# Up projections of one SwiGLU layer by Strassen's seven products instead of eight

## The chip, the cores and the metric

The kernel runs on one core of a Trainium2 chip. The metric is the device time of one execution in microseconds (us); smaller is better. Five engines work side by side, each through its own list of instructions in order, and meet at semaphores: PE (TensorE, matrix products, with its weight loads shown as PEld), DVE (VectorE), ACT (ScalarE), POOL (GpSimd) and SP (SyncE, which here only issues DMAs).

## The reference

Two trunk layers work on 256 context tokens and 512 latent tokens of 1024 channels. Each layer is a half-step SwiGLU, a mixer (attention beside a convolution in the first layer, a two-way RWKV-7 scan in the second) and another half-step SwiGLU. The change concerns the first SwiGLU of the second layer, for all 768 tokens:

```python
def half_ffn(x, shift, scale, gate, w1, w3, w2):
    h = modulate(x, shift, scale)
    return x + 0.5 * gate * ((jax.nn.silu(h @ w1) * (h @ w3)) @ w2)
```

`w1` and `w3` are 1024 x 2816, `w2` is 2816 x 1024.

## The kernel before

All activations lie with channels on the 128 lanes and tokens along the row, so 1024 channels are 8 tiles (k) and the 2816 inner channels 22 blocks of 128 (f). The tokens form two groups, CTX (columns 0 to 255) and LAT (256 to 767).

Products are made in three parts. Every operand is split into a high part, rounded by a copy to a shorter float type, and a low part, the rest; `mmk` (L435) issues high x high, high x low and low x high into the same PSUM bank. For a weight tile (128 x 1024) the split is a copy on ACT (`whi`, L202) and a subtraction on DVE (`wlo`, L209). The pool of weights holds four raw tiles and four split pairs (`W_RAW`, `W_SP`). PSUM has eight banks, four called `psa` and four called `psb`.

In `ffn` (L469), `f1` makes one block f: 48 products with a `w1` tile (8 k x 3 parts x 2 groups), SiLU on ACT (L476), 48 products with the `w3` tile, and for each group the gate: a product on DVE (`fs`, L484), a rounded copy on ACT (`ghi`, L485) and the rest on DVE (`glo`, L486). `f2` brings a chunk of blocks down: for each of eight output tiles m and each group `down` (L503) multiplies the chunk's gated blocks with `w2` and adds the result to the residual on DVE (L511). Chunks are 4, 4, 4, 4, 2 and 4 blocks; a chunk's `f2` runs after the first block of the next chunk. The very first two blocks of the layer run k by k while the normalisation still delivers (`first_block`).

The order of everything is written out by hand: each engine executes its instructions in the order in which the Python emits them. `w_next` (L211) emits the split of later weight tiles ahead of the block that now starts. `ticks` (L181) emits one piece of background work at a time; in this layer there is none before the change.

Of the kernel before, what the change touches and what calls it, by code (L numbers as in the profile page):

```python
# [7 lines left out]
F32 = mybir.dt.float32  # L8
F32R = mybir.dt.float32r
# [12 lines left out]
CHUNKS = (4, 4, 4, 4, 2, 4)  # L22
CTX = (0, NCTX, 1)
# [6 lines left out]
class Cols:  # L30
    def __init__(self):
        self.at = {}
        self.n = 0
# [56 lines left out]
def layout(inp):  # L90
# [10 lines left out]
    parts, f0 = [], 0  # L101
    for cf in CHUNKS:
        t = w2[:, :, f0:f0 + cf].reshape(2, 2, cf, 128, cf, 8 // cf, 128)
        parts.append(t.transpose(0, 1, 4, 3, 5, 2, 6).reshape(2, 2, -1))
        f0 += cf
    a["w2"] = np.ascontiguousarray(np.concatenate(parts, 2))
# [33 lines left out]

class K:
# [10 lines left out]
    # ---------- pools  # L152
# [33 lines left out]
    # ---------- weights  # L186
# [24 lines left out]
    def w_next(self, key, live=0):  # L211
        i = self.w_i
        assert self.w_items[i][0] == key, (self.w_items[i][0], key)
        last = min(i + self.W_SP - 1 - live - 1, len(self.w_items) - 1)
        while self.w_s <= max(last, i):
            while self.w_d <= min(self.w_s + self.W_RAW - 1, len(self.w_items) - 1):
# [4 lines left out]
        while self.w_d <= min(self.w_s + self.W_RAW - 1, len(self.w_items) - 1):  # L221
            self.w_dma(self.w_d)
            self.w_d += 1
# [30 lines left out]
    # ---------- adaLN  # L254
# [17 lines left out]
    def ada_first(self):  # L272
        """shift and scale of the first FFN, half of the channels at a time: every product on the tensor engine, four column groups at once"""
# [53 lines left out]
    # ---------- norm + modulation: h = x * rsqrt(mean(x^2) + eps) * scale + shift  # L327
# [89 lines left out]
    # ---------- SwiGLU  # L417
    def ffn_items(self, l, i):
        A = self.A
        it = []  # L420
        off = f = 0
# [47 lines left out]
    def ffn(self, l, i, groups, h, post=None, first=None):  # L469
        nc = self.nc  # L470
        gd = 2 if i == 0 else 8
        gs = {}

# [14 lines left out]
        def f1(f, nt):  # L488
# [6 lines left out]
            w = self.w_next(("w3", l, i, f))  # L495
            pss = [self.psa() for g in groups]
# [27 lines left out]
        for c, cf in enumerate(CHUNKS):  # L524
            q = 0
            if c == 0 and first is not None:
# [54 lines left out]
                q = 2  # L581
            while q < cf:
# [10 lines left out]
        c, f0, cf = pend  # L593
        if post is None:
            f2(c, f0, cf)
            return None
# [29 lines left out]
    # ---------- MLA || conv mixer  # L626
# [18 lines left out]
    def conv_tap(self, t, k, split=False):  # L645
        """one tap of the depthwise convolution; zeros part the two streams in cin"""
# [20 lines left out]
    def mla(self, h, norm_lat):  # L667
# [54 lines left out]
        # the first two blocks of the convolution's input run while the latent tokens are normalised  # L722
# [34 lines left out]
        # latent projections: kv, q, rope key  # L757
# [58 lines left out]
        # token-major q, k, v  # L816
# [11 lines left out]
        def rot(dst, src, w, t, n, eng):  # L828
            """gain and rotation of n tables' tokens; src and dst [128, n, 32], t the first table, or None where nothing turns"""
# [27 lines left out]
        def prep(p):  # L857
            """closures: transposes, split and row maxima of one pair of heads"""
# [129 lines left out]
        self.plan(self.wout_items() + self.ffn_items(0, 1) + self.ffn_items(1, 0) + self.rwkv_items())  # L988
# [72 lines left out]
        def fin(p):  # L1061
            """closures: one over the sums, and the outputs split"""
# [181 lines left out]
        # output projection  # L1244
# [16 lines left out]
        # the attention's half of the rows first; the first NH blocks of the latent tokens go with the context's  # L1261
# [45 lines left out]
    # ---------- RWKV-7 mixer (second layer)  # L1307
# [22 lines left out]
    def rw_sum(self, kt, g):  # L1330
        """the sum of a token's neighbours"""
# [10 lines left out]
    def rw_diff(self, kt, g):  # L1342
        """half the sum, less the token"""
# [1394 lines left out]
```

## Time and profile before

| quantity | value |
|---|---|
| median of 3 timed runs | 3436.01 us (3432.27 to 3439.86) |
| span of the profiled execution | 3438.3 us, within the timed runs |
| matrix products on PE | 21064 |
| mean granted PE clock | 0.947 |

The profile covers one execution from the first to the last instruction; its span is the time that the sums below refer to, 2.3 us above the median. A line of a group names the source line, the engine, the operation, the output and input tiles by the program's names, the shape, how often it ran and its mean duration. In a line of the timeline the first number is the start in us from the span's start, the second the duration.

### The profile page before, as it was taken

The page shows a single profiled execution, that of the slowest core. Times are in us where ns is not written, and L with a number is a line of the kernel's source. Part 1 is how long each engine was busy: PE and PEld are TensorE (multiplying, and loading weights), DVE is VectorE, ACT ScalarE, POOL GpSimd, SP SyncE. Part 2 cuts the span into 40 slices and gives each one's busy share as a digit, 9 for nine tenths or more (in the row PEclk, how much of TensorE's full clock was granted, in tenths as well). Part 3 has the DMA queues.
Part 4 walks back from the last instruction along what each step waited for, and adds up shares of the span by engine and source line. Part 5 has one row for each costly group of instructions (what it writes and reads, how often), then busy time and mean ns, then how long its engine had stood idle before and what let it go on. Part 6 is the DMA issues. An engine that isn't in the chain of part 4 may idle for free. (4 is left out here: it accounts for less than half of the span.)

```text
span 3438.3 us, 51746 instructions
## 1 busy us (share of the span) xinstructions
PE 3168.0 (92%) x21064; PEld 2636.7 (77%) x21064; DVE 2069.5 (60%) x3246; ACT 1141.4 (33%) x2060; POOL 663.6 (19%) x464
## 2 busy tenths in 40 slices
PE   7999999988989999999999999998786477789999
PEld 6888888874578888888888888776554367678887
DVE  5877734798667776555333343637899775663443
ACT  4122213455543211124122113335564245532222
POOL 1000001356320000002000001215787142230000
PEclk9999999999999999999999999999777689989999
DMA  6444311200133444431111111322587788733222
GB/s 242 146 150 147 132 68 62 78 25 1 47 108 129 141 140 150 146 111 56 68 62 62 62 68 62 109 89 95 149 213 201 186 186 184 165 127 103 98 98 80
DMA packets 251374, 390.59 MB, mean 114 GB/s; under 512 B 67328, under 2 KB 136576, under 8 KB 251136
## 3 DMA queue, kind: packets, MB, share of 16 engines
q1 hardware_dynamic: 251136, 387.28, 36.7%
q8 instruction: 166, 2.72, 0.3%
q14 instruction: 72, 0.59, 0.1%
HBM read 323.24 MB, written 63.96 MB: 113 GB/s over the span
## 5 line engine op out<-in xcount | busy, mean ns | idle before, releaser
L233 PE MATMUL psa<-hhi,whi 128*128 128x512 f32 (+1 forms) x2584 | 893.5, 346 | 6.0 <-ACT whi L202 3.9
L233 PE MATMUL psa<-hlo,whi 128*128 128x512 f32 (+1 forms) x2584 | 894.8, 346 | 2.5 <-POOL hlo L385 2.2
L233 PE MATMUL psa<-hhi,wlo 128*128 128x512 f32 (+1 forms) x2584 | 892.1, 345 | 0.0
L209 DVE TENSOR_TENSOR wlo<-wraw,whi 128x1024 fp32r<-128x1024 f32 (+3 forms) x300 | 366.9, 1225 | 450.5 <-ACT whi L202 450.5
L233 PEld LDWEIGHTS psa<-hhi,whi 128*128 128x128 f32 x2584 | 490.0, 190 | 69.7 <-ACT whi L202 3.9
L233 PEld LDWEIGHTS psa<-hlo,whi 128*128 128x128 f32 x2584 | 489.2, 189 | 67.1 <-POOL hlo L385 4.1
L233 PEld LDWEIGHTS psa<-hhi,wlo 128*128 128x128 f32 x2584 | 489.6, 189 | 61.3
L202 ACT CAST whi<-wraw 128x1024 fp32r<-128x1024 f32 (+2 forms) x345 | 344.6, 1009 | 337.1 <-PE psb L233 198.2
L233 PE MATMUL psb<-ghi,whi 128*128 128x512 f32 (+1 forms) x1232 | 425.6, 345 | 1.4 <-DVE xb L511 0.9
L233 PE MATMUL psb<-glo,whi 128*128 128x512 f32 (+1 forms) x1232 | 424.8, 345 | 0.0
L233 PE MATMUL psb<-ghi,wlo 128*128 128x512 f32 (+1 forms) x1232 | 424.5, 345 | 0.0
L342 POOL TENSOR_TENSOR nacc<-nacc,nsq 128x512 f32<-128x512 f32 (+1 forms) x50 | 56.2, 1125 | 1579.0 <-ACT nsq L338 1574.0
L476 ACT ACTIVATE fs<-psa 128x512 f32<-128x512 f32 (+1 forms) x152 | 77.3, 509 | 576.3 <-PE psa L233 576.2
L485 ACT CAST ghi<-fs 128x512 fp32r<-128x512 f32 (+1 forms) x154 | 81.7, 530 | 552.7 <-DVE fs L484 552.7
L233 PEld LDWEIGHTS psb<-ghi,whi 128*128 128x128 f32 x1232 | 231.9, 188 | 32.8 <-issue 2.2
L233 PEld LDWEIGHTS psb<-ghi,wlo 128*128 128x128 f32 x1232 | 232.0, 188 | 30.0
L233 PEld LDWEIGHTS psb<-glo,whi 128*128 128x128 f32 x1232 | 231.8, 188 | 30.0 <-DVE glo L486 0.3
L484 DVE TENSOR_TENSOR fs<-fs,psa 128x512 f32<-128x512 f32 (+1 forms) x149 | 85.1, 571 | 200.5 <-PE psa L233 197.5
L511 DVE SCALAR_TENSOR_TENSOR xb<-psb,mod,xb 128x256 f32<-128x256 f32 (+1 forms) x192 | 115.7, 614 | 124.5 <-PE psb L233 124.4
L268 DVE CUSTOM_DVE_ANT_0 adaj<-adat,sc,vec 128x512 bf16<-128x512 f32 x224 | 167.9, 750 | 14.7 <-DMA adat<-ada 9.1
L268 DVE CUSTOM_DVE_ANT_0 adaj<-adat,sc,mod 128x512 bf16<-128x512 f32 x224 | 167.9, 750 | 5.9 <-DMA adat<-ada 0.3
L233 PE MATMUL psb<-rhs,lhs 96*32 96x64 f32 (+1 forms) x2560 | 81.1, 241 | 70.4 <-DVE prod L2104 21.4
(398 smaller groups left out, 4907.7 us busy)
## 6 DMA issues: line engine op xcount, KB each, us to landing
wraw<-w SPq DMA_DIRECT2D x264, 512.0 KB
adat<-ada SPq DMA_DIRECT2D x256, 256.0 KB
la_d<-AR SPq DMA_DIRECT2D x32, 384.0 KB
kb_d<-KT SPq DMA_DIRECT2D x16, 768.0 KB
lg_d<-G SPq DMA_DIRECT2D x32, 384.0 KB
lhs<-la_d SPq DMA_DIRECT2D x48, 256.0 KB
lhs<-lg_d SPq DMA_DIRECT2D x48, 256.0 KB
kb<-kb_d SPq DMA_DIRECT2D x48, 256.0 KB
```

The costliest lines, as they stand in the source:

```text
L202: nc.scalar.copy(hi, raw)
L209: nc.vector.tensor_tensor(lo, raw, hi, ALU.subtract)
L233: self.last = self.nc.tensor.matmul(ps, lhsT=lhsT, rhs=rhs, start=start, stop=stop)
L268: nc.vector.tensor_tensor_reduce(out=junk, in0=t, in1=self.sc[cd][hf], scale=1.0, scalar=o if hf else self.col("ada_b", l * 72 + j), op0=A ...
L342: (eng or nc.gpsimd).tensor_tensor(st["acc"], st["acc"], sq, ALU.add)
L476: nc.scalar.activation(s, ps[:, 0:grp[1]], AF.Silu)
L484: nc.vector.tensor_tensor(s, s, ps[:, 0:n], ALU.mult)
L485: nc.scalar.copy(ghi[:, t0:t0 + n], s)
L511: nc.vector.scalar_tensor_tensor(xs, ps[:, 0:n], self.modc(l, gd, m, cd), xs, ALU.mult, ALU.add)
```

## The change

The 18 blocks from f = 4 on are taken in nine pairs. For a pair and one of `w1`, `w3` the product has two halves of inner channels (the two blocks), two halves of input channels (k 0 to 3 and 4 to 7) and two halves of tokens (columns 0 to 383 and 384 to 767, slices tA and tB). The class `Strassen` forms it from seven products of half size in place of eight. Each of the seven is 12 matrix products (4 k x 3 parts) of 384 columns into one `psa` bank, and is named in `ORDER` after its token operand.

- Token operands: `sums` adds and subtracts the four quarters of the activations once and splits the results; S2, S3 and A22 go to new tiles `ht2`, `ht3`, `ht4` as background work during blocks 2 and 3, S1 overwrites part of the activations during the first products (`one`).
- Weight operands: per pair and matrix, four subtractions or additions of 128 x 512 on DVE (L226 to L229) change the raw tiles, and the splits (L234, L237) make three and a half 1024-wide units instead of two. `ahead` emits one unit ahead of each product when fewer than four are held.
- Results: `pair` combines the seven products on DVE (seven additions of 384 columns, `add`, L358) and by one copy on ACT (L369); `out` applies SiLU and the gate to each of four quarters of the pair (L345, L353 to L355).
- Down projection: chunks are now pairs of blocks (`PAIRS`), and the eight steps m of the previous pair's down projection stand among the 14 products of a pair, behind the products listed in `STEPS`. The same `w2` bytes are packed two blocks to a tile (array `w2p`); two `w2` units are split per pair.

The rows below are instructions as they stand in the two programs, with the semaphores on which each waits in brackets. Before, on DVE, this is a block's `w3` half and the first three steps of the down projection behind it (`xb`: the residual tiles, two rows a step, CTX and LAT):

```order
L209 TENSOR_TENSOR wlo<-wraw,whi 128x1024 [waits DMAHW1_49,Activation_49]
L484 TENSOR_TENSOR fs<-fs,psa 128x256 [waits PE_49]
L486 TENSOR_TENSOR glo<-fs,ghi 128x256 [waits Activation_49]
L484 TENSOR_TENSOR fs<-fs,psa 128x512 [waits PE_49]
L486 TENSOR_TENSOR glo<-fs,ghi 128x512 [waits Activation_49]
L209 TENSOR_TENSOR wlo<-wraw,whi 128x1024 [waits DMAHW2_49,Activation_49]
L511 SCALAR_TENSOR_TENSOR xb_7779<-psb,mod_83,xb_7779 128x256 [waits PE_49]
L511 SCALAR_TENSOR_TENSOR xb_7779<-psb,mod_83,xb_7779 128x512 [waits PE_49]
L511 SCALAR_TENSOR_TENSOR xb_7781<-psb,mod_83,xb_7781 128x256 [waits PE_49]
L511 SCALAR_TENSOR_TENSOR xb_7781<-psb,mod_83,xb_7781 128x512 [waits PE_49]
L209 TENSOR_TENSOR wlo<-wraw,whi 128x1024 [waits DMAHW3_49,Activation_49]
L511 SCALAR_TENSOR_TENSOR xb_7783<-psb,mod_83,xb_7783 128x256 [waits PE_49]
```

After, on DVE, the `w3` half of a pair in the run of pairs. The first row adds product S2; `wlo` is a `w2` unit of the next pair; then come the addition for S3, the evictions of a step, two additions for S1 with gate product and rest (`glo`), and the next step's evictions:

```order
L358 TENSOR_TENSOR e<-psa,e 128x384 [waits PE_49]
L237 TENSOR_TENSOR wlo<-wraw,whi 128x1024 [waits DMAHW6_49,PE_49,Activation_49]
L358 TENSOR_TENSOR e<-psa,e 128x384 [waits DVE_49]
L792 SCALAR_TENSOR_TENSOR xb_7789<-psb,mod_83,xb_7789 128x256
L792 SCALAR_TENSOR_TENSOR xb_7789<-psb,mod_83,xb_7789 128x512
L358 TENSOR_TENSOR e<-psa,e 128x384 [waits DVE_49]
L358 TENSOR_TENSOR e<-psa,e 128x384
L353 TENSOR_TENSOR e<-e 128x384 [waits DVE_49]
L355 TENSOR_TENSOR glo<-e,ghi 128x384 [waits Activation_49]
L792 SCALAR_TENSOR_TENSOR xb_7791<-psb,mod_83,xb_7791 128x256
L792 SCALAR_TENSOR_TENSOR xb_7791<-psb,mod_83,xb_7791 128x512
```

The rest of the same half: the four sums of the next weights, the addition for A22 with its gate, a `wlo`, and the addition for S4 with its gate:

```order
L226 TENSOR_TENSOR ws_15418<-wraw 128x512 [waits DMAHW5_49]
L227 TENSOR_TENSOR wraw<-wraw 128x512 [waits DVE_49]
L228 TENSOR_TENSOR wraw<-ws_15418,wraw 128x512 [waits DVE_49]
L229 TENSOR_TENSOR wraw<-wraw 128x512 [waits DVE_49]
L358 TENSOR_TENSOR e<-psa,e 128x384
L353 TENSOR_TENSOR e<-e 128x384 [waits DVE_49]
L355 TENSOR_TENSOR glo<-e,ghi 128x384 [waits Activation_49]
L237 TENSOR_TENSOR wlo<-wraw,whi 128x1024 [waits PE_49]
L358 TENSOR_TENSOR e<-psa,e 128x384
L353 TENSOR_TENSOR e<-e 128x384 [waits DVE_49]
L355 TENSOR_TENSOR glo<-e,ghi 128x384 [waits Activation_49]
```

Against before, the additions and the gates have come between the splits, and each group of rows stands behind a `wlo` row that waits for PE.

Before, on PE, the end of a block's LAT products and the start of the down projection:

```order
L233 MATMUL psa<-hlo_13643,whi 128x512
L233 MATMUL psa<-hhi_13635,wlo 128x512
L233 MATMUL psb<-ghi,whi 128x256 [waits Activation_49]
L233 MATMUL psb<-glo,whi 128x256
L233 MATMUL psb<-ghi,wlo 128x256 [waits DVE_49]
L233 MATMUL psb<-ghi,whi 128x256
```

After, on PE, the end of product A12 of a pair (`hhi`, 384 columns) and the first step of the previous pair's down projection; the two `psb` groups are CTX and LAT, and within a group the two blocks of the pair:

```order
L506 MATMUL psa<-hhi_13635,wlo 128x384
L506 MATMUL psb<-ghi,whi 128x256 [waits DVE_49,Activation_49]
L506 MATMUL psb<-glo,whi 128x256
L506 MATMUL psb<-ghi,wlo 128x256
L506 MATMUL psb<-ghi,whi 128x256 [waits Activation_49]
L506 MATMUL psb<-glo,whi 128x256 [waits DVE_49]
L506 MATMUL psb<-ghi,wlo 128x256
L506 MATMUL psb<-ghi,whi 128x512 [waits Activation_49]
L506 MATMUL psb<-glo,whi 128x512 [waits DVE_49]
```

Before, the gate for which the first step waits belongs to a block with another whole block of products between; now the last one belongs to S4 of the pair just finished, with one step, A11 and A12 between on PE.

The diff, cut to its core (removed comments, the packing of `w2p`, the lists of items and of loads, and a smaller scratch area for DMA descriptors, which makes room in SBUF, are left out):

```diff
 CHUNKS = (4, 4, 4, 4, 2, 4)
+PAIRS = (2, 2, 2, 2, 2, 2, 2, 2, 2, 4)
...
+class Strassen:
+    PLACE = {"A11": (0, 0), "A12": (0, 1), "S2": (1, 0), "S4": (1, 1), "S3": (2, 0), "A22": (2, 1), "S1": (3, 0)}
+    ORDER = "A11", "A12", "S2", "S3", "S1", "A22", "S4"
+    STEPS = 1, 3, 4, 6, 8, 10, 11, 13
+    def __init__(self, k, l, i, groups, h, gs):
+        self.k, self.nc, self.h, self.gs = k, k.nc, h, gs
+        A = k.A
+        c0 = groups[0][0]
+        n = self.n = sum(g[1] for g in groups) // 2
+        self.tt = [slice(c0, c0 + n), slice(c0 + n, c0 + 2 * n)]
+        self.fp, self.close = k.open("fx", 1, side="right")
+        self.T = {}
+        self.mats = [(m, f) for f in range(4, NF, 2) for m in ("w1", "w3")]
...
+        self.units, self.loads = [], []
+        for j, (m, f) in enumerate(self.mats):
+            self.units += [(j, 0), (j, 1), (j, 2), (j, 3)]
+            self.loads += [((j, q), A[m][l, i, f + q].rearrange("p k m -> p (k m)")) for q in range(2)]
+            c = f // 2 - 1
+            if c < len(PAIRS) - 1:
+                key = ("w2", c, j % 2)
+                self.units.insert(len(self.units) - 3, key)
+                self.loads.append((key, w2[key[1:]]))
...
+    def split(self):
+        nc, k = self.nc, self.k
+        u = self.units[self.u]
+        self.u += 1
+        TT = nc.vector.tensor_tensor
+        if u[0] != "w2" and u[1] == 3:
+            hi = self.fp.tile([128, 512], F32R, tag="hi", bufs=1, name="shi")
+            lo = self.fp.tile([128, 512], F32R, tag="lo", bufs=1, name="slo")
+        else:
+            hi = k.wp.tile([128, 1024], F32R, tag="hi", bufs=k.W_SP, name="whi")
+            lo = k.wp.tile([128, 1024], F32R, tag="lo", bufs=k.W_SP, name="wlo")
+        self.sp[u] = hi, lo
+        drop = []
+        if u[0] == "w2":
+            x = self.raw[u]
+            drop = [u]
+        else:
+            j, q = u
+            if q == 1:
+                R0, R1 = self.raw[j, 0], self.raw[j, 1]
+                s1 = self.tmp[j] = k.tp.tile([128, 512], F32, tag="t", name="ws1")
+                TT(s1, R1[:, 0:512], R1[:, 512:1024], ALU.add)
+                TT(R1[:, 0:512], R0[:, 0:512], R1[:, 0:512], ALU.subtract)
+                TT(R0[:, 0:512], s1, R0[:, 0:512], ALU.subtract)
+                TT(R0[:, 512:1024], R0[:, 512:1024], R0[:, 0:512], ALU.subtract)
+            x = {0: self.raw.get((j, 0)), 1: self.raw.get((j, 0)), 2: self.raw.get((j, 1)), 3: self.tmp.get(j)}[q]
+            drop = {0: [], 1: [(j, 0)], 2: [(j, 1)], 3: []}[q]
+            if q == 3:
+                del self.tmp[j]
+        nc.scalar.copy(hi, x)
+        def f():
+            TT(lo, x, hi, ALU.subtract)
+            for r in drop:
+                del self.raw[r]
+        return f
+    def ahead(self):
+        self.flush()
+        self.load()
+        if self.u < len(self.units):
+            u = self.units[self.u]
+            small = [v for v in self.sp if v[1] == 3 and v[0] != "w2"]
+            if (not small) if (u[0] != "w2" and u[1] == 3) else len(self.sp) - len(small) < self.k.W_SP:
+                self.late = [self.split()]
...
+    def unit(self, u, last):
+        while self.u <= self.at[u]:
+            self.flush()
+            self.load()
+            self.late = [self.split()]
+        if self.at[u] == self.u - 1:
+            self.flush()
+        return self.sp.pop(u) if last else self.sp[u]
+    def sums(self):
...
+        def plain(kt, c):
+            t = et()
+            TT(t, hhi[kt][:, c], hlo[kt][:, c], ALU.add)
+            return t
+        def split(x, hi, lo):
+            nc.scalar.copy(hi, x)
+            TT(lo, x, hi, ALU.subtract)
+        def s1(kt):
+            tiles[kt] = [plain(kt, tA), plain(kt, tB), plain(kt + 4, tA), plain(kt + 4, tB)]
+        def s2(kt):
+            r11, r12, r21, r22 = tiles[kt]
+            TT(r11, r12, r11, ALU.subtract)
+            TT(r12, r22, r12, ALU.subtract)
+            TT(r22, r22, r11, ALU.subtract)
+            TT(r21, r21, r22, ALU.subtract)
+        def s3(kt):
+            r11, r12, r21, r22 = tiles.pop(kt)
+            for o, x in ((2, r22), (3, r12), (4, r21)):
+                t = k.slab([128, NT], F32R, f"ht{o}")
+                self.T[o, kt] = t[:, 0:n], t[:, n:2 * n]
+                split(x, *self.T[o, kt])
+        k.bg += [lambda f=f, kt=kt: f(kt) for kt in range(4) for f in (s1, s2, s3)]
+        def one(kt):
+            a, b = plain(kt, tA), plain(kt, tB)
+            TT(b, b, a, ALU.subtract)
+            split(b, hhi[kt][:, tB], hlo[kt][:, tB])
+        self.one = [lambda kt=kt: one(kt) for kt in range(4)]
...
+    def product(self, j, o):
+        k = self.k
+        u, q = self.PLACE[o]
+        hi, lo = self.unit((j, u), o in ("A12", "S1", "A22", "S4"))
+        c = slice(512 * q, 512 * q + 512)
+        w = hi[:, c], lo[:, c]
+        hi = lo = None
+        self.ahead()
+        ps = k.psa()
+        for kt in range(4):
+            k.mmk(ps[:, 0:self.n], w, kt, self.rhs(o, kt), kt == 0, kt == 3)
+        return ps
...
+    def out(self, j, blk, x):
+        nc, k = self.nc, self.k
+        m, f = self.mats[j]
+        if m == "w1":
+            nc.scalar.activation(x, x, AF.Silu)
+            self.s[blk] = x
+            return
+        s = self.s.pop(blk)
+        f += blk[0]
+        if f not in self.gs:
+            self.gs[f] = (k.slab([128, NT], F32R, "ghi"), k.slab([128, NT], F32R, "glo"))
+        hi, lo = (t[:, self.tt[blk[1]]] for t in self.gs[f])
+        nc.vector.tensor_tensor(s, s, x, ALU.mult)
+        nc.scalar.copy(hi, s)
+        nc.vector.tensor_tensor(lo, s, hi, ALU.subtract)
...
+    def pair(self, f, step):
+        at = 0
+        for m in ("w1", "w3"):
+            j = self.mats.index((m, f))
+            for o in self.ORDER:
+                ps = self.product(j, o)
+                if o == "A11":
+                    u2 = self.e()
+                    self.nc.scalar.copy(u2, ps[:, 0:self.n])
+                elif o == "A12":
+                    c11 = self.e()
+                    self.add(c11, ps, u2)
+                    self.out(j, (0, 0), c11)
+                    c11 = None
+                elif o == "S2":
+                    self.add(u2, ps, u2)
+                elif o == "S3":
+                    u3 = self.e()
+                    self.add(u3, ps, u2)
+                elif o == "S1":
+                    c22 = self.e()
+                    self.add(c22, ps, u3)
+                    self.add(u2, ps, u2)
+                    self.out(j, (1, 1), c22)
+                    c22 = None
+                elif o == "A22":
+                    self.add(u3, ps, u3)
+                    self.out(j, (1, 0), u3)
+                    u3 = None
+                else:
+                    self.add(u2, ps, u2)
+                    self.out(j, (0, 1), u2)
+                    u2 = None
+                ps = None
+                if self.one:
+                    self.one.pop(0)()
+                if step and at in self.STEPS:
+                    step(self.STEPS.index(at))
+                at += 1
+    def end(self):
+        self.flush()
+        self.T.clear()
+        self.load()
+        self.k.w_pre()()
+        self.k.w_pre()()
+        self.close()
...
             w = self.w_next(("w3", l, i, f))
+            if fast and f == 3:
+                fx.begin()
...
-        for c, cf in enumerate(CHUNKS):
+        chunks = PAIRS if fast else CHUNKS
+        w2w = []
+        def step(c, f0, m):
+            if m % 4 == 0:
+                w2w.clear()
+                w2w.append(fx.unit(("w2", c, m // 4), True))
+            for g in groups:
+                down(f0, 2, m, w2w[0], g)
+            if m == 7:
+                w2w.clear()
+                for f in range(f0, f0 + 2):
+                    del gs[f]
+        for c, cf in enumerate(chunks):
+            if fast and c > 1:
+                for f in range(f0, f0 + cf, 2):
+                    if pend:
+                        fx.pair(f, lambda m, c=pend[0], q=pend[1]: step(c, q, m))
+                    else:
+                        fx.pair(f, None)
+                    pend = None
+                pend = (c, f0, cf)
+                f0 += cf
+                continue
...
                 q = 2
+                if fast:
+                    fx.sums()
...
         c, f0, cf = pend
+        if fast:
+            fx.end()
         if post is None:
...
-        self.plan(self.wout_items() + self.ffn_items(0, 1) + self.ffn_items(1, 0) + self.rwkv_items())
+        self.plan(self.wout_items() + self.ffn_items(0, 1))
+        it, tail = self.ffn_items(1, 0, True)
+        self.plan(it)
+        self.w_stops.append(len(self.w_items))
+        self.plan(tail + self.rwkv_items())
...
-        st = self.ffn(1, 0, [CTX, LAT], h, post=self.rw_begin, first=self.hook(st0, 1, 0, h))
+        st = self.ffn(1, 0, [CTX, LAT], h, post=self.rw_begin, first=self.hook(st0, 1, 0, h), fast=True)
...
```

More of the change, by code (lines that the diff above doesn't have):

```diff
@@ L138, in layout, with load, flush, begin @@
     return a
+class Strassen:
[11 more added lines that the diff above has]
+        self.mats = [(m, f) for f in range(4, NF, 2) for m in ("w1", "w3")]
+        w2, off = {}, 0
+        for c, cf in enumerate(PAIRS):
+            for b in range(cf):
+                w2[c, b] = A["w2p"][off:off + 131072].rearrange("(p n) -> p n", p=128)
+                off += 131072
+        self.units, self.loads = [], []
[7 more added lines that the diff above has]
+                self.loads.append((key, w2[key[1:]]))
+        self.at = {u: n for n, u in enumerate(self.units)}
+        self.u = 0
+        self.raw, self.tmp, self.sp = {}, {}, {}
+        self.late = []
+        self.s = {}
+    def load(self):
+        k = self.k
+        while self.loads and len(self.raw) < k.W_RAW:
+            key, ap = self.loads.pop(0)
+            t = self.raw[key] = k.wp.tile([128, 1024], F32, tag="raw", bufs=k.W_RAW, name="wraw")
+            self.nc.sync.dma_start(out=t, in_=ap)
+        if not self.loads:
+            while k.w_d < len(k.w_items) and k.w_d - k.w_s + len(self.raw) < k.W_RAW:
+                k.w_dma(k.w_d)
+                k.w_d += 1
+    def split(self):
[33 more added lines that the diff above has]
+        return f
+    def flush(self):
+        while self.late:
+            self.late.pop(0)()
+    def ahead(self):
[6 more added lines that the diff above has]
+                self.late = [self.split()]
+    def begin(self):
+        for _ in range(2):
+            self.ahead()
[8 more added lines that the diff above has]
+    def sums(self):
+        k, nc = self.k, self.nc
+        hhi, hlo = self.h
+        n = self.n
+        tA, tB = self.tt
+        TT = nc.vector.tensor_tensor
+        tiles = {}
+        def et():
+            return self.fp.tile([128, n], F32, tag="e", bufs=7, name="e")
+        def plain(kt, c):
[25 more added lines that the diff above has]
+        self.one = [lambda kt=kt: one(kt) for kt in range(4)]
+    def rhs(self, o, kt):
+        hhi, hlo = self.h
+        tA, tB = self.tt
+        k, c = {"A11": (kt, tA), "A12": (kt + 4, tA), "S4": (kt + 4, tB), "S1": (kt, tB), "S2": (2, None), "S3": (3, None), "A22": (4, None)}[o]
+        if c is None:
+            return self.T[k, kt]
+        return hhi[k][:, c], hlo[k][:, c]
+    def product(self, j, o):
+        k = self.k
+        u, q = self.PLACE[o]
[3 more added lines that the diff above has]
+        hi = lo = None
+        self.ahead()
+        ps = k.psa()
+        for kt in range(4):
+            k.mmk(ps[:, 0:self.n], w, kt, self.rhs(o, kt), kt == 0, kt == 3)
+        return ps
+    def e(self):
+        return self.fp.tile([128, self.n], F32, tag="e", bufs=7, name="e")
+    def out(self, j, blk, x):
[13 more added lines that the diff above has]
+        nc.vector.tensor_tensor(lo, s, hi, ALU.subtract)
+    def add(self, out, ps, x):
+        self.nc.vector.tensor_tensor(out, ps[:, 0:self.n], x, ALU.add)
+    def pair(self, f, step):
[44 more added lines that the diff above has]
+        self.close()
@@ L214, in w_next @@
         last = min(i + self.W_SP - 1 - live - 1, len(self.w_items) - 1)
+        stops = self.w_stops
+        while stops and i >= stops[0]:
+            stops.pop(0)
+        end = min(len(self.w_items), stops[0] if stops else 1 << 30)
+        last = min(last, end - 1)
         while self.w_s <= max(last, i):
-            while self.w_d <= min(self.w_s + self.W_RAW - 1, len(self.w_items) - 1):
+            while self.w_d <= min(self.w_s + self.W_RAW - 1, end - 1):
                 self.w_dma(self.w_d)
@@ L624, in ffn, with strassen @@
         return sts[-1]
+    def strassen(self, l, i, groups, h, gs):
+        return Strassen(self, l, i, groups, h, gs)
     def mla_items(self):
```

30 lines of the change are left out of this document (20 added, 10 removed).

## The prediction

> **What bounds the kernel now.** The page comes first: PE is busy for 92% of the span, nine tenths or ten in slices 20 to 24, where the changed layer lies.
>
> ```profile
> span 3438.3 us, 51746 instructions
> PE 3168.0 (92%) x21064; PEld 2636.7 (77%) x21064; DVE 2069.5 (60%) x3246; ACT 1141.4 (33%) x2060; POOL 663.6 (19%) x464
> ```
>
> Then the view by stretches, of a hundred us inside the layer: PE has no gap, DVE works a third of the time, the clock is full.
>
> ```profile
> core 0: us, PE busy (x) PEld busy (x) DVE busy (x) ACT busy (x) POOL busy (x), PEclk, DMA share, GB/s
> 1700.00:1800.00 100.00, 100.00 (x575) 87.64 (x574) 32.73 (x44) 19.73 (x28) 0.00 (x0) 1.00 0.18 63
> ```
>
> So PE alone sets the time here, and each microsecond taken from it or added to it as a wait counts in full. The timeline of ACT gives PE's pace, since SiLU starts when a group's products end (CTX, LAT, then CTX of the next block):
>
> ```profile
> 1632.27 0.39 ACT L476 ACTIVATE fs<-psa 128x256 f32<-128x256 f32 x1 [0.52 <-PE psa L233]
> 1637.84 0.60 ACT L476 ACTIVATE fs<-psa 128x512 f32<-128x512 f32 x1 [5.18 <-PE psa L233]
> 1649.07 0.39 ACT L476 ACTIVATE fs<-psa 128x256 f32<-128x256 f32 x1 [0.52 <-PE psa L233]
> ```
>
> 24 LAT products take 5.57 us, 0.232 each. A block (two matrices, 48 products of 512 and 48 of 256 columns) takes 16.80, which leaves 0.118 for 256 columns. For 384 columns I take the middle, 0.175. Before the change two blocks cost 33.6 us up and 16.8 down (the same 48 + 48 products), 50.4 together.
>
> **What goes.** A product of Strassen's is 12 x 0.175 = 2.10 us; a step of the down projection (6 x 0.118 + 6 x 0.232) also 2.10. I call this a slot. A pair needs 14 + 8 = 22 slots, 46.2 us, against 24. That saves 4.2 us a pair, 37.8 for nine, if PE never waits. The Trainium skill (TensorE: Matmul & The Clock Gate, "Wait — 56ns, not 53.3ns?") gives N / 2.4 GHz + 2.5 ns from start to start, by which the saving would be 35.1 us; the rows are some 8% slower than that, and I keep the rows.
>
> **What comes.** The durations on DVE and ACT are those of this layer (groups by shape, 1640 to 2040):
>
> ```profile
> L209 DVE TENSOR_TENSOR wlo<-wraw,whi 128x1024 fp32r<-128x1024 f32 x48 | 58.7, 1222 | 113.8 <-ACT whi L202 113.8
> L202 ACT CAST whi<-wraw 128x1024 fp32r<-128x1024 f32 x47 | 48.9, 1048 | 78.1 <-PE psb L233 58.4 <-issue 19.7
> L511 DVE SCALAR_TENSOR_TENSOR xb<-psb,mod,xb 128x512 f32<-128x512 f32 x32 | 24.0, 750 | 60.4 <-PE psb L233 60.4
> L511 DVE SCALAR_TENSOR_TENSOR xb<-psb,mod,xb 128x256 f32<-128x256 f32 x32 | 15.4, 481 | 10.7 <-PE psb L233 10.7
> L486 DVE TENSOR_TENSOR glo<-fs,ghi 128x512 fp32r<-128x512 f32 x16 | 11.1, 692 | 11.0 <-ACT ghi L485 11.0
> L484 DVE TENSOR_TENSOR fs<-fs,psa 128x512 f32<-128x512 f32 x16 | 11.0, 688 | 68.0 <-PE psa L233 68.0
> L485 ACT CAST ghi<-fs 128x512 fp32r<-128x512 f32 x16 | 10.0, 623 | 86.8 <-DVE fs L484 86.8
> L486 DVE TENSOR_TENSOR glo<-fs,ghi 128x256 fp32r<-128x256 f32 x16 | 6.8, 425 | 7.6 <-ACT ghi L485 7.6
> L484 DVE TENSOR_TENSOR fs<-fs,psa 128x256 f32<-128x256 f32 x16 | 6.7, 421 | 0.3
> L485 ACT CAST ghi<-fs 128x256 fp32r<-128x256 f32 x16 | 6.5, 408 | 27.6 <-DVE fs L484 27.6
> ```
>
> A 384-wide DVE operation is then 0.56 us (bounds 0.42 and 0.69), a 384-wide copy on ACT 0.52, an addition of two 128 x 512 weight halves 0.69. In a pair DVE has 8 `wlo` (9.8 us), 2 small ones and 8 weight sums (6.9), 14 additions (7.8), 4 gates (4.5) and 16 evictions (9.8): 38.8 of 46.2 us. The total fits; the order doesn't. How operations follow each other:
>
> ```profile
> 1705.53 1.22 DVE L209 TENSOR_TENSOR wlo<-wraw,whi 128x1024 fp32r<-128x1024 f32 x1
> 1706.66 0.48 DVE L511 SCALAR_TENSOR_TENSOR xb<-psb,mod,xb 128x256 f32<-128x256 f32 x1
> 1723.20 1.23 DVE L209 TENSOR_TENSOR wlo<-wraw,whi 128x1024 fp32r<-128x1024 f32 x1 [8.09 <-ACT whi L202]
> 1724.47 0.42 DVE L484 TENSOR_TENSOR fs<-fs,psa 128x256 f32<-128x256 f32 x1
> 1725.36 0.42 DVE L486 TENSOR_TENSOR glo<-fs,ghi 128x256 fp32r<-128x256 f32 x1 [0.47 <-ACT ghi L485]
> ```
>
> Where nothing is waited for, the next starts 0.08 before the last one's end (1706.66); a result handed to another engine costs 0.03 or so (0.47 from `fs` to `glo`, of which ACT holds 0.41).
>
> The new wait is this. There are four split pairs. When product S3 begins, they hold the `w2` tile in use (four steps long), the unit of S2 and S4, the unit of S3 and A22, and the next A11's unit. The `w2` unit of the next half is split right then; the first tile to come free is that of S3 and A22, at the end of A22. So ACT's copy and DVE's `wlo` wait for the end of A22, while behind `wlo` on DVE stand the addition for S3, the evictions of a step, both additions for S1, and all that follows (the rows of DVE in the last section).
>
> From the end of A22 in a `w3` half (time 0), in the order of the rows: copy to 1.1, `wlo` 2.3, S3 added 2.8, evictions of step 5 at 3.2 and 3.9, two additions 4.8, gate of (1,1) 5.3, 5.9 (ACT) and 6.4, evictions of step 6 at 7.5, four weight sums (each needs the one before) 10.3, A22 added 10.8, its gate 11.4, 12.0 (ACT, behind a 1.05 copy) and 12.5, `wlo` 13.7, S4 added 14.2, its gate 14.8, `ghi` 15.3, `glo` 15.9. PE meanwhile: S4 to 2.1; step 7 needs the bank that step 5's first eviction frees, so it runs from 3.2 to 5.3 (**1.1 lost**); the next pair's A11 to 7.4, A12 to 9.5; then step 0, which multiplies the gates just made: its CTX half needs the gate of A22 (12.0 and 12.5), its LAT half that of S4 (15.3 and 15.9). It ends five products after 15.9, at 17.1 instead of 11.6: **5.5 lost**. With both ends of the 384-wide operations (eleven on this path, 0.14 either way) it is 4.0 to 7.0. In a `w1` half there is no gate; the same hold costs 1.1 at step 3, and DVE is level again before the next A22.
>
> Over the layer: 1.1 x 8 at step 7, 1.1 x 7 at step 3 (the first pair has another order there), 5.5 x 7 at step 0: 8.8 + 7.7 + 38.5 = 55.0.
>
> **The ends of the run.** The sums of the activations are 44 operations of 384 columns, some 23 us on DVE during blocks 2 and 3. DVE is free from here on:
>
> ```profile
> 1631.78 1.23 DVE L209 TENSOR_TENSOR wlo<-wraw,whi 128x1024 fp32r<-128x1024 f32 x1 [0.27 <-ACT whi L202]
> ```
>
> that is 3.7 us after block 2 starts (1632.27 less 24 x 0.118 and a lag). Two of four lots (5.9 each), two `wlo` and the gates bring it to 20.9 at the first eviction of chunk 0's down projection, which PE began at 16.8. PE can be two steps ahead (four `psb` banks). The other two lots lie among the evictions, and step 7 may start only after eviction 5, at 38.1, instead of 31.5: 6.5 lost. In the first pair, S2 waits for its unit (four sums, one lot of S1's operand, `wlo`: until 10.0 after the pair's start instead of 6.7), S3 likewise, S1 for its own operand: 3.3 + 3.3 + 1.3 = 7.9. In the last pair, without steps, the additions for A12 wait behind the weight sums and A22 waits for their bank: 3.5. Then the tail's first `w2` tile is split only behind the last gate (copy to 2.9, `wlo` 4.1 after S4): 4.1. Together 22.0; from nothing to a third more, 0 to 29.
>
> **The clock.** After the norm's one-column products (1592.2 to 1594.9) the granted clock fell:
>
> ```profile
> 1594.34 0.58 PE L233 MATMUL psa<-cs,nsq 128*128 128x1 f32 x4
> 1595.00:1596.00 1.00, 1.00 (x8) 0.71 0.92 369
> 1596.00:1597.00 1.00, 1.00 (x7) 0.50 0.18 70
> 1597.00:1598.00 1.00, 1.00 (x6) 0.50 0.00 0
> 1598.00:1599.00 1.00, 1.00 (x8) 0.58 0.00 0
> ```
>
> The missing shares add to 1.7 us. Step 0's two waits (2.2 and 2.5 us idle, little between) and two in the first pair are like it: nine places, 0 to 1.7 each; part of a dip falls on the wait itself, so I take half, 8 us. The Trainium skill (TensorE: Matmul & The Clock Gate, "What's actually happening") has the clock at half after one idle window of about 3.4 us; by that rule each step 0, with six almost idle us, pays in full, which is the third rival.
>
> **The sum** is 55.0 + 22.0 + 8 - 37.8 = +47 us on the execution of 3438.3, which lies 2.3 above the median; on the median's scale 3436 + 47 = **3483**. DMA is no term: as many `w2` bytes, at 0.18 of the queues' time.
>
> **Rivals.** (1) The hold isn't there: a `w2` unit finds a tile free before A22 ends, say that of A12. Then DVE's 38.8 us spread over 46.2, no step waits, and only the ends remain: -37.8 + 22 = -16, 3420, faster. It decides at the copy of the `w2` unit: S4's gate must be done 9 to 10 us after A22, not 15.9. The count of tiles and DVE's wait for PE in that row speak against it. (2) The hold is there, but step 0 hardly waits, since ACT and DVE overlap better than the rows say: 55 becomes 16.5, without the clock's 8: about 3437, no change; stretched over the bounds of 384-wide operations, 3437 to 3455. The five gates and additions after A22 need each other, which speaks against it. (3) Every wait at step 0 halves the clock for one or two windows: 9 x 1.7 to 9 x 3.4 in place of 8, 3490 to 3506. (4) DVE becomes the bound outright: 38.8 a pair is below both 46.2 and 50.4, so no.
>
> **Chances.** The forecast 0.64, with 3460 to 3490; rival 3 0.16; rival 2 0.12, half of it within 0.2%; rival 1 0.08. The terms' bounds (step 0 by 10 either way, the ends 22 down to 7 up, the clock 8) added by squares give 24; the range is 3450 to 3506, which leaves out rivals 1 and most of 2. Faster by over 0.2% (7 us, about what a measurement of this kernel can tell from no change): 0.08; within: 0.07; slower: 0.85.
>
> **What would show it.** In the changed profile: 384-wide products 0.175 apart; PE's waits for `ghi` and `glo` some 5 us a pair, in seven groups 54 us apart; DVE idle up to 9 us ahead of a `wlo` that ACT's copy releases, that copy waiting for PE; DVE's share in the layer up from a third to 0.7. The forecast is wrong if the pairs repeat every 46 to 48 us (rival 1), or if the waits at step 0 are under 2 us (rival 2).

## The result and the profile after

The changed kernel takes 3489.11 us (median of 4 runs, 3485.00 to 3492.14) against 3435.23 (4 runs, 3432.27 to 3439.86): the ratio is 1.0155, 95% interval 1.0141 to 1.0169, so some 54 us slower. Forecast were 3483 and +47. The page of the profiled execution begins:

```profile
span 3487.5 us, 51779 instructions
PE 3168.4 (91%) x20848; PEld 2658.9 (76%) x20848; DVE 2268.5 (65%) x3604; ACT 1180.5 (34%) x2130; POOL 665.1 (19%) x464
```

PE has 216 products fewer than before and the same busy time: what the products save is taken again, partly as slower products. To see where, the layer is cut at PE's own rows. First, by stretches of PE, the whole layer from block 2 to the mixer's first product, and then the rest of the program (stretch; its length, PE busy and number of products; granted clock; DMA), before:

```profile
1629.18:2152.96 523.78, 522.21 (x2989) 1.00 0.18 64
2152.96:3438.30 1285.34, 1079.30 (x9113) 0.89 0.51 139
```

The same after, cut finer: blocks 2 and 3 with chunk 0's down projection, the first pair, the seven pairs behind it, the last pair, and the down projection of the last four blocks:

```profile
1627.75:1686.21 58.46, 53.16 (x290) 0.97 0.12 41
1686.21:1742.19 55.98, 50.88 (x265) 0.91 0.19 66
1742.19:2133.40 391.21, 348.26 (x1849) 0.95 0.16 57
2133.40:2166.48 33.08, 30.39 (x169) 1.00 0.14 48
2166.48:2211.16 44.68, 39.70 (x205) 0.89 0.22 77
sum 583.41, PE 522.39; mean PE 104.48
```

The layer has become 583.41 - 523.78 = 59.6 us longer. Seven pairs at 46.2 would be 323.4; they take 67.8 more, 9.7 each. The rest of the program, in which nothing was meant to change, is 9.0 us shorter (3487.5 - 2211.16 = 1276.3 against 1285.3), and the start 1.4. The execution profiled before was a long one: a span lies some 1.7 us under the time of its execution (3487.5 against 3489.22), so 3438.3 stands for some 3440, 4.8 above the median of 3435.23. On the medians (53.9 longer) the part outside the layer is 59.6 - 53.9 = 5.7 us. In the executions profiled here that rest takes between 1274 and 1285 us, whatever is done in the layer; it is not explained, and the layer's own time is the better measure in what follows.

What PE waits for in the layer, three rows of the view of waits (us in total, times, longest):

```profile
PE psb L506 <- ACT ghi L354: 27.2, 14, 2.2
PE psb L506 <- DVE xb L792: 20.6, 19, 2.3
PE psb L506 <- DVE glo L355: 1.5, 7, 0.2
```

`ghi` and `glo` are step 0's gates, in seven groups of two; of the 19 waits for `xb`, 15 of 1.02 us are those at step 3 and step 7, the others stand at chunk 0. One of the groups in the timeline of PE (start, duration, then in brackets the idle time before and who ended it): step 7, then step 0 of the next pair in three pieces.

```profile
1796.01 0.39 PE L506 MATMUL psb<-ghi,whi 128*128 128x256 f32 x1 [1.02 <-DVE xb L792]
1804.63 0.39 PE L506 MATMUL psb<-ghi,whi 128*128 128x256 f32 x1 [1.72 <-ACT ghi L354]
1805.23 0.39 PE L506 MATMUL psb<-glo,whi 128*128 128x256 f32 x1 [0.21 <-DVE glo L355]
1807.96 0.63 PE L506 MATMUL psb<-ghi,whi 128*128 128x512 f32 x1 [2.24 <-ACT ghi L354]
```

ACT's timeline at the same place shows what went before. The first copy is that of the `w2` unit:

```profile
1792.79 1.05 ACT L234 CAST whi<-wraw 128x1024 fp32r<-128x1024 f32 x1 [8.52 <-PE psa L506]
1798.04 0.51 ACT L354 CAST ghi<-e 128x384 fp32r<-128x384 f32 x1 [4.20 <-DVE e L353]
1803.06 1.04 ACT L234 CAST whi<-wraw 128x1024 fp32r<-128x1024 f32 x1 [4.51 <-DVE wraw L229]
1804.07 0.51 ACT L354 CAST ghi<-e 128x384 fp32r<-128x384 f32 x1
```

And DVE's: `wlo` released by that copy, and at the end the addition for S4, its gate product and `glo`:

```profile
1793.87 1.22 DVE L237 TENSOR_TENSOR wlo<-wraw,whi 128x1024 fp32r<-128x1024 f32 x1 [6.36 <-ACT whi L234]
...
1806.22 0.55 DVE L358 TENSOR_TENSOR e<-psa,e 128x384 f32<-128x384 f32 x1
1806.81 0.56 DVE L353 TENSOR_TENSOR e<-e 128x384 f32<-128x384 f32 x1
1807.94 0.56 DVE L355 TENSOR_TENSOR glo<-e,ghi 128x384 fp32r<-128x384 f32 x1 [0.58 <-ACT ghi L354]
```

DVE had been idle for 6.36 us, and then is late with everything. A22 ended at 1792.7; `glo` of S4 is done at 1808.5, 15.8 us later, where the prediction's chain gave 15.9.

Behind the wait, the clock, at step 0 of the next pair: first the 3.41 us before the clock falls, then some windows of a us:

```profile
1859.37:1862.78 3.41, 0.89 (x3) 1.00 0.03 5
1863.00:1864.00 1.00, 0.61 (x2) 0.50 0.84 324
1866.00:1867.00 1.00, 1.00 (x5) 0.50 0.00 0
1869.00:1870.00 1.00, 1.00 (x6) 0.70 0.00 0
1870.00:1871.00 1.00, 1.00 (x8) 1.00 0.00 0
```

PE is at half speed for nearly 7 us, and fully busy from 1864 to 1869: products of 512 columns start 0.43 us apart there (1865.00, 1865.42, 1865.85), where 0.232 is usual.

### The profile page after: what moved, and what is told of

The parts are those of the page before. It is cut to its first block, busy times and chain, and to the rows that moved or that the text cites. A ratio compares the mean times of both kernels' runs of the same rounds, so it can differ in the third digit from the quotient of the medians.

```text
span 3487.5 us, 51779 instructions
## 1 busy us (share of the span) xinstructions
PE 3168.4 (91%) x20848; PEld 2658.9 (76%) x20848; DVE 2268.5 (65%) x3604; ACT 1180.5 (34%) x2130; POOL 665.1 (19%) x464
## 5 line engine op out<-in xcount | busy, mean ns | idle before, releaser
L506 PE MATMUL psa<-hhi,whi 128*128 128x512 f32 (+2 forms) x2224 | 772.7, 347 | 6.2 <-ACT whi L470 3.9
L506 PE MATMUL psa<-hlo,whi 128*128 128x512 f32 (+2 forms) x2224 | 773.8, 348 | 2.5 <-POOL hlo L658 2.3
L506 PE MATMUL psa<-hhi,wlo 128*128 128x512 f32 (+2 forms) x2224 | 771.6, 347 | 0.0
L477 DVE TENSOR_TENSOR wlo<-wraw,whi 128x1024 fp32r<-128x1024 f32 (+2 forms) x246 | 301.0, 1226 | 305.7 <-ACT whi L470 305.6
L506 PE MATMUL psb<-ghi,whi 128*128 128x256 f32 (+1 forms) x1232 | 435.5, 353 | 51.9 <-ACT ghi L354 27.2
L506 PE MATMUL psb<-glo,whi 128*128 128x256 f32 (+1 forms) x1232 | 432.9, 351 | 1.5 <-DVE glo L355 1.5
L506 PE MATMUL psb<-ghi,wlo 128*128 128x256 f32 (+1 forms) x1232 | 430.9, 350 | 0.7 <-DVE wlo L475 0.7
L470 ACT CAST whi<-wraw 128x1024 fp32r<-128x1024 f32 (+3 forms) x293 | 290.0, 1001 | 254.2 <-PE psb L506 125.4
L792 DVE SCALAR_TENSOR_TENSOR xb<-psb,mod,xb 128x256 f32<-128x256 f32 (+1 forms) x256 | 149.2, 611 | 56.6 <-PE psb L506 56.5
L237 DVE TENSOR_TENSOR wlo<-wraw,whi 128x1024 fp32r<-128x1024 f32 x70 | 85.3, 1219 | 143.0 <-ACT whi L234 143.0
L234 ACT CAST whi<-wraw 128x1024 fp32r<-128x1024 f32 x70 | 73.1, 1046 | 232.0 <-PE psa L506 160.3
```

The lines of the kernel that those rows point to most:

```text
L234: nc.scalar.copy(hi, x)
L237: TT(lo, x, hi, ALU.subtract)
L470: nc.scalar.copy(hi, raw)
L477: nc.vector.tensor_tensor(lo, raw, hi, ALU.subtract)
L506: self.last = self.nc.tensor.matmul(ps, lhsT=lhsT, rhs=rhs, start=start, stop=stop)
L792: nc.vector.scalar_tensor_tensor(xs, ps[:, 0:n], self.modc(l, gd, m, cd), xs, ALU.mult, ALU.add)
```

## The experiments

Theory H is the prediction's: the `w2` unit is split while all four pairs are held, and the in-order queues of ACT and DVE stand until A22 ends. Against it stood that the chain from S4 to step 0 is too long in itself (G), and that DVE has too much to do (D). Each kernel is the changed one with the edit shown (e5 and e6 have e1's as well), and was compared with the kernel before on the same chip.

**e1_count: the hold taken away.** The lead counts a `w2` tile as free as soon as step 0 or 4 has fetched it, although three more steps read it. The edit counts it as held, and lets go of it behind the last step that reads it (3 or 7):

```diff
-            if (not small) if (u[0] != "w2" and u[1] == 3) else len(self.sp) - len(small) < self.k.W_SP:
+            if (not small) if (u[0] != "w2" and u[1] == 3) else len(self.sp) - len(small) + self.held < self.k.W_SP:
...
                 w2w.append(fx.unit(("w2", c, m // 4), True))
+                fx.held = 1
...
+            if m % 4 == 3:
+                w2w.clear()
+                fx.held = 0
             if m == 7:
-                w2w.clear()
```

> The lead of the weight splits counts the w2 tile that the steps still use as one of the four pairs, so the w2 unit of the next half is split behind the additions for A22 and not ahead of those for S3. Nothing is computed otherwise. Theory H (the hold on the in-order queues is the cause): the pairs repeat every 46.2 to 47 us instead of 55.9, seven times 9.7 = 68 us and some 4 us at step 7 of the first pair and in the last pair go: 3489 - 72 = 3417, 3410 to 3425. Rival G (the chain of addition, gate and split from S4 to step 0 is too long in itself): step 0 still waits, pairs of 52 us or more, 3460 or above. Rival D (VectorE has too much to do): pairs of 50 us, 3448.

Measured: 3423.52 us (6 runs), ratio 0.9957 (0.9940 to 0.9974) to the kernel before: some 0.4% faster than it, and 66 us less than the changed kernel. By stretches of PE, the first pair, the seven pairs and the last:

```profile
1689.98:1744.05 54.07, 48.73 (x266) 0.97 0.17 59
1744.05:2068.41 324.36, 324.31 (x1850) 1.00 0.21 69
2068.41:2097.81 29.40, 29.40 (x169) 1.00 0.22 72
```

Seven pairs take 324.36, 46.34 each, against 50.4 for two blocks before; PE doesn't wait in them and the clock stays at 1.00. The layer takes 508.4 us, 75.0 less than in the changed kernel, 66.9 of it in the seven pairs; start and rest of the program were 10 us longer in this execution. What DVE waits for in the pairs, in the changed kernel:

```profile
DVE wlo L237 <- ACT whi L234: 121.9, 21, 11.0
DVE glo L355 <- ACT ghi L354: 16.2, 28, 0.6
DVE e L358 <- PE psa L506: 1.5, 3, 0.7
```

and in this one:

```profile
DVE e L359 <- PE psa L507: 34.5, 34, 1.4
DVE glo L356 <- ACT ghi L355: 15.9, 27, 0.8
DVE wlo L238 <- ACT whi L235: 2.8, 7, 0.4
```

The wait for the copy goes from 121.9 us to 2.8, and DVE now waits for products, which means that it is ahead of PE. G and D fall: neither the chain nor the load was changed, only the place of one split in the queue and the moment at which a tile is let go.

**e2_late_step: step 0 moved away from the gates, the hold kept.**

```diff
-    STEPS = 1, 3, 4, 6, 8, 10, 11, 13
+    STEPS = 3, 4, 5, 6, 8, 10, 11, 13
```

> The first three steps stand one or two products later (behind products 3, 4 and 5 in place of 1, 3 and 4), the hold is left as it is. Rival G: step 0 now comes two slots, 4.2 us, later, which is all of its idle time of 4.1 us; without idle time no half clock either, 7 x 7.7 = 54 us go: 3435. Theory H: VectorE is as late as before, and what waits is the next thing in its queue, the weight units for S2 and S3: at most a third of it is won, 3470 to 3490.

Measured: 3480.87 us (4 runs), ratio 1.0132 (1.0113 to 1.0150). Only 8 us are won (9.1 in the layer), although no step waits for a gate any more. In PE's waits in the layer stands instead:

```profile
PE psa L506 <- DVE wlo L237: 23.2, 16, 2.0
PE psa L506 <- ACT whi L234: 14.1, 8, 3.0
PE psb L506 <- DVE xb L792: 13.4, 12, 2.3
```

The lateness of the two queues is the cause, and the gate only the first thing to meet it: with that cover the weight units of the next products are late.

**e3_a12_twice: more work in the wait.**

```diff
-        for kt in range(4):
-            k.mmk(ps[:, 0:self.n], w, kt, self.rhs(o, kt), kt == 0, kt == 3)
+        for _ in range(2 if o == "A12" and j % 2 == 0 else 1):
+            for kt in range(4):
+                k.mmk(ps[:, 0:self.n], w, kt, self.rhs(o, kt), kt == 0, kt == 3)
```

> Product A12 of every w1 half is issued twice into the same bank (the second starts the sum anew), 12 more products of 2.1 us in all, right ahead of step 0, which waits 4.1 us there anyway. If the half clock comes from the idle stretch (5.9 us at half speed per pair, 2.9 us lost), the shorter stretch brings one window or none: 7 x (1.2 to 2.9) = 8 to 20 us faster than the changed kernel, 3469 to 3481, with more work done. If the clock is nothing to do with the idle stretch: 3489 within 3 us, the work being hidden in the wait. If the wait was not a wait for the gates: 9 x 2.1 = 19 us slower, 3508.

Measured: 3487.83 us (4 runs, 3478.08 to 3497.86): by the time alone it can't be told from no change, and the 8 to 20 us don't show in it. The layer shows more. From the copy of A11 in the second pair to that in the last, PE by stretches in the changed kernel:

```profile
1752.32:2141.19 388.87, 350.08 (x1863) 0.95 0.17 58
```

and here:

```profile
1753.16:2135.56 382.40, 353.76 (x1935) 0.98 0.18 59
```

With 12 more products in each, the seven periods are 6.5 us shorter, and the granted clock is 0.98 in place of 0.95: of 388.9 us some 19 were missing, of 382.4 some 8. The shorter stretch without work did keep the clock up in part of the pairs: it fell behind four of the seven step 0s. Counted on PE from A11 to A11, the three periods without a drop take 54.1 to 54.2 us, the three with 3.4 us of half clock 55.2 to 55.3, and the one with 6.8 us 56.6. The first and the last pair, by stretches of PE:

```profile
1687.66:1743.04 55.38, 49.46 (x278) 1.00 0.20 67
2127.78:2160.85 33.07, 32.16 (x181) 1.00 0.14 48
```

They took 55.98 and 33.08 in the changed kernel, so the doubled product makes neither longer: in the last pair it lies in the wait for a bank (2.4 us before, 0.9 now), and in the first the clock, 0.91 there, stays at 1.00. The layer takes 573.7 us, 9.7 less than in the changed kernel: 6.5 in the seven pairs, a little under what was expected, 0.6 in the first, and 2.7 in the tail, where nothing was changed. Start and rest of the program were 5.2 us longer in this execution, and the four times lie 20 us apart, which is why the whole doesn't show it. That A12's doubling lies in a wait, and that the clock hangs on the idle stretch, is what the profiled execution shows.

**e4_lo_pool and e7_lo_late: which queue stands.** e4 gives the subtraction of the `w2` units to GpSimd, e7 leaves it on DVE and issues it three products later; in both ACT's copy stays where it was.

```diff
-            TT(lo, x, hi, ALU.subtract)
+            (nc.gpsimd if u[0] == "w2" else nc.vector).tensor_tensor(lo, x, hi, ALU.subtract)
```

> The subtraction of the w2 units goes from VectorE to GpSimd; ACT's copy of the same units still waits for the end of A22, and the units that a product needs next are as before. Theory H in the form that it is VectorE's queue behind wlo that makes step 0 late: the additions and evictions no longer stand behind it, the gates are late only by what ACT's copy holds up on ACT, pairs of 48 to 50 us instead of 55.9: 3489 - 7 x (6 to 8) = 3433 to 3447. If ACT's queue alone makes it late: no gain, 3480 to 3490.

Measured: 3465.54 us (4 runs), ratio 1.0088 (1.0066 to 1.0110), the pairs 52.2 us apart (by the copies of A11 on ACT; 55.6 in the changed kernel): a third of the hold's price is won, which lies between what the two forms of the theory gave. The diff of e7 (a counter of three products, which then issues the subtraction; a step that needs it sooner issues it itself):

```diff
+                if u[0] == "w2":
+                    self.wait.append([3, self.late.pop()])
...
+        if self.wait:
+            self.wait[0][0] -= 1
+            if self.wait[0][0] == 0:
+                self.wait.pop(0)[1]()
```

> The changed kernel with VectorE's wlo of the w2 units issued three products later (behind the wait it used to stand in), all on VectorE; ACT's copy still waits for the end of A22. VectorE's queue no longer stands, ACT's does, and GpSimd is not used. If it was GpSimd's hold of VectorE that left e4_lo_pool at pairs of 52.2 us: pairs of 49 to 50. If it is ACT's copy, behind which the copy of the (1,1) gate stands for which VectorE then waits: pairs of 51 to 53, step 7 no longer waiting and step 0 still.

Measured: 3457.25 us (one run), pairs 51.0 us apart, PE waiting at step 0 but no longer at step 7, as expected if ACT's copy counts. In the first pair the edit itself makes a step wait 8.6 us for a subtraction that comes too late, so that the distance of the pairs says more than the time. ACT in e7, the copy and behind it that of the (1,1) gate:

```profile
1788.09 1.05 ACT L235 CAST whi<-wraw 128x1024 fp32r<-128x1024 f32 x1 [10.73 <-PE psa L515]
1789.05 0.51 ACT L363 CAST ghi<-e 128x384 fp32r<-128x384 f32 x1
```

So the hold acts through both queues: of its price about half goes when DVE's place is mended, and the rest only when the copy on ACT is moved as well (e1). The 1.2 us a pair between e4 and e7 fit GpSimd's hold of DVE in the last section, but the two also order `wlo` differently, so that they are not shown to be its alone.

**e5_ends and e6_ends_pool: the ends of the run, on top of e1.** Both take the sums of the activations away from chunk 0's first steps, split one unit more ahead of the first pair and the tail's first `w2` tiles during the last pair; e5 also makes the operands of S1 two at a time:

```diff
-        for _ in range(2):
+        for _ in range(3):
             self.ahead()
...
+        elif self.pre < 2 and not self.loads and len(self.sp) - len([v for v in self.sp if v[1] == 3]) + self.pre < self.k.W_SP:
+            f = self.k.w_pre()
+            if f:
+                self.late = [f]
+                self.pre += 1
...
-                self.ticks(1)
+                self.ticks(1 if not fast or m >= 4 else 0)
```

> On top of e1_count the ends of the run: the activation sums put nothing among the first four steps of chunk 0's down projection, one more weight unit is split ahead of the first pair, the operands of S1 are made two at a time, and the tail's first two w2 tiles are split during the last pair instead of behind its last gate. Theory E (the ends cost what PE waits there): of e1's 8.1 us at chunk 0, 7.9 in the first pair and 5.2 in the tail go 5, 2 and 5: 3423 - 12 = 3411, 3406 to 3416. Rival: the work only moves, VectorE has too much of it in these blocks whatever the order, and the next product waits as long: 3420 to 3424.

Measured: 3408.16 us (4 runs, 3400.45 to 3415.56), ratio 0.9914 (0.9891 to 0.9936): 15 us under e1, of which the layer gives 9.0 (508.4 in e1). By stretches of PE:

```profile
1627.17:1681.57 54.40, 52.09 (x289) 0.97 0.16 54
1681.57:1733.62 52.05, 48.15 (x266) 0.97 0.16 51
1733.62:2057.90 324.28, 324.28 (x1850) 1.00 0.21 69
2057.90:2087.30 29.40, 29.40 (x170) 1.00 0.32 108
2087.30:2126.57 39.27, 36.98 (x206) 0.96 0.17 61
sum 499.40, PE 490.90; mean PE 98.18
```

Chunk 0's stage has 4.0 us too much left (8.1 in e1), the first pair 5.9 (7.9), the tail is 2.8 us shorter (42.10 in e1); the waits became shorter and did not only move. Of the 5, 2 and 5 us that were expected, 4.1, 2.0 and 2.8 came; the remaining 6 us of the 15 lie outside the layer. e6 puts the additions on GpSimd, leaves none of the sums among chunk 0's steps and makes S1's operands one at a time:

```diff
-            TT(t, hhi[kt][:, c], hlo[kt][:, c], ALU.add)
+            k.ptt(t, hhi[kt][:, c], hlo[kt][:, c], ALU.add)
...
-            TT(b, b, a, ALU.subtract)
+            k.ptt(b, b, a, ALU.subtract)
```

> As e5_ends, but the 24 plain additions of the activation sums, and the four subtractions for S1, are done by GpSimd, which is idle here, and none of the sums stands among the steps of chunk 0 (S1's operands one at a time). If GpSimd works beside VectorE: VectorE has 28 operations of 0.56 us less, the waits at chunk 0 and in the first pair fall to some 1 and 2 us: 3405. If VectorE stands still while GpSimd works, as one subtraction of 384 columns did in e4_lo_pool (2.49 us in place of 0.56, ending 0.4 us behind GpSimd's), the 28 cost more on GpSimd (0.9 us each, estimated from its 1.12 for 128x512) than they did on VectorE: nothing won against e5_ends or some 5 us lost, 3411 to 3420.

Measured: 3413.71 us (4 runs, 3407.93 to 3420.84), ratio 0.9930 (0.9913 to 0.9948). Nothing is won against e5; whether something is lost the two intervals leave open. In the executions profiled the layer takes 503.0 us, 3.6 more than in e5, but the two also order the sums differently. The 1.12 us of the expectation is the mean of a group of two shapes (1.48 for 128x512 and 0.74 for 128x256); GpSimd's additions of 384 columns took 1.0 to 2.0 us here. It speaks against a GpSimd that works beside DVE at no cost.

## Why the prediction was right, and where it wasn't

The saving is what was forecast: a pair without waits takes 46.3 us (e1) where 46.2 was said, and a pair without steps 29.40, 14 products of 2.10.

The hold is there, at the place and through the engines that the prediction named: taken away (e1) it gives 66 us back (75 in the layer), moved (e2) it comes out elsewhere. Its waits at steps 3 and 7 were priced at 1.1 us and show 1.02 of idle time. Step 0's delay was priced at 5.5: with step 7 starting at 1796.01, step 0 would start three slots later, at 1802.3, and end at 1804.4; `glo` of S4 is done at 1808.5, and five products of 0.232 at full clock end at 1809.7, 5.3 later. The three periods of e3 without a drop of the clock show the waits alone: they take 7.9 to 8.0 us more than 46.2, where 1.1 + 1.1 + 5.5 = 7.7 had been priced. DVE's load was put at 38.8 us a pair; the durations in the seven pairs add up to 38.9 a pair, but DVE is busy for 35.6 (249.4 in all), because operations that wait for nothing start 0.08 us before the end of the one ahead of them; nothing hung on that.

The ends came near their sizes: 6.5 for chunk 0 (58.46 less three times 16.8 is 8.1, in which 0.03 of the clock, 1.8, is what the term didn't have), 3.5 for the last pair (33.08 - 29.40 = 3.7), 4.1 for the tail's first tile (3.25 + 0.66 of idle time). The first pair was given 7.9, one step 7 and two dips, 10.7, and took 9.8 more than 46.2, but with shorter waits (5.1 us of idle time) and a clock of 0.91: two errors that nearly cancel.

The step that failed is the clock's. "Part of a dip falls on the wait itself, so I take half, 8 us" was too little: it took one dip of 1.7 us for each place, and the profile shows half speed for 3.4 or 6.8 us behind every step 0. Of the 9.7 us that a pair loses, 1.2 + 1.2 + 5.3 are waits (idle time and the end of the product before it) and some 2 the products that then run slowly, against 0.85. Over seven pairs that is 8 us more; in the tail, to which no dip had been given, 3.7 more (44.68 against 36.93 before is 7.8 in place of 4.1); at chunk 0 1.6 and in the last pair 0.2; with the first pair's 0.9 less together the 12.6 by which the layer's 59.6 exceeds 47. That is the third rival's size, and in the layer it was the third rival that came true, not the forecast. The tail's share isn't fixed by its waits: in e1, with the same wait of 3.25 us at its start, the half clock lasts 3.4 us in place of 10.2 and the tail takes 42.1. The rule of the Trainium skill that stood beside it (TensorE: Matmul & The Clock Gate, "What's actually happening": half clock after one idle window of about 3.4 us) agrees with the length of the drops (3.41 or 6.83 us) and with e1, where nothing waits and the clock stays at 1.00. It doesn't agree in one point, and there the traces decide: the window need not be idle throughout, for PE was busy during 0.9 to 1.7 us of the 3.41 before each of the seven drops.

The layer alone would have given 3435.2 + 59.6 = 3494.8. That the median is 3489.11, 0.9 us under the 3490 that parts the forecast from the third rival, is luck: outside the layer the medians are 5.7 us closer, which nobody forecast and which stays open. The range begins at 3450, although the bounds of the terms, 24 us, give 3459; nothing hung on that either.

Rivals 1 and 2 are out. For the second, step 0 would have had to wait under 2 us, and it has 4.1 us of idle time in each of the seven groups (27.2 + 1.5 together). The first describes e1, the kernel in which the hold really is absent, and had 3420 for it (3423.5 measured).

## What to carry to other kernels

A lead that counts buffers must count the ones still being read: a split issued one place too early on an in-order queue doesn't start early, it stops all that is behind it, here 66 us for a change that needed no new work. When a product is made cheaper on an engine that never waited, look first for the first wait that the new order creates, and price it together with the slow clock behind it. And when a wait is seen at one instruction, ask whether its engine's whole queue is late: moving the instruction then only moves the wait.

## What the runs showed of the hardware that was not expected

A DVE operation that reads two tiles in SBUF stands still while GpSimd works. In e4 GpSimd's subtraction:

```profile
1788.02 2.39 POOL L237 TENSOR_TENSOR wlo<-wraw,whi 128x1024 fp32r<-128x1024 f32 x1 [20.36 <-ACT whi L234]
```

and the operation that DVE began 0.3 us later:

```profile
1788.33 2.49 DVE L355 TENSOR_TENSOR glo<-e,ghi 128x384 fp32r<-128x384 f32 x1 [4.06 <-ACT ghi L354]
```

It takes 2.49 us where 0.56 is usual, and ends 0.4 us behind GpSimd's; the same stands in seven pairs (2.49 to 2.50 us). The Trainium skill (SBUF — State Buffer, "Who interferes with whom") says that the two engines share one pair of ports under an exclusive lock; this row agrees. The same subtraction takes GpSimd 2.39 us and DVE 1.22. An operation that reads PSUM and one tile in SBUF isn't held: in the other half of a pair one of 0.55 us, as usual, lies within GpSimd's subtraction:

```profile
1764.95 2.71 POOL L237 TENSOR_TENSOR wlo<-wraw,whi 128x1024 fp32r<-128x1024 f32 x1 [26.27 <-ACT whi L234]
1765.31 0.55 DVE L358 TENSOR_TENSOR e<-psa,e 128x384 f32<-128x384 f32 x1
```

The clock moves in steps of 3.41 us, and where a wait falls among them goes with whether it costs a dip; no edit tested that. In e3 the clock falls at 1752.64, 1861.87, 1971.09 and 2080.32, each 109.23 us, or 32 times 3.413, behind the one before. In the 3.41 us before these four drops PE is idle for 1.7 to 2.2 us. At the other three step 0s of e3 the same idle time, some 2.4 us in all, lies across the end of a step, 1.3 to 1.6 us on one side and 0.8 to 1.1 on the other, and the clock stays up. How much idle time in a step is needed isn't shown more closely: in the changed kernel 1.7 us was followed by a drop at one place (2084.65) and by none at another (chunk 0).
